# Holding the transfers on GpSimd's queue behind cells, cutting the casting copies into shorter runs, and adding identity products to the head of a matmul-GELU-matmul kernel

## The chip, the cores and the metric

The kernel runs on one core of one Trainium2 chip. The metric is the device time of one launch in microseconds (us), as the median of several launches. A core has five instruction streams that run beside each other: TensorE (PE in the profile, with its weight loads as PEld), VectorE (DVE), ScalarE (ACT), GpSimd (POOL) and SyncE (SP, which here issues DMA transfers alone). Each stream works off its own instructions in the order in which they stand, and waits for another stream or a transfer only where the instruction in front needs it.

## The reference

```python
def reference(x, w1, b1, w2):          # x 16x512x768, w1 768x3072, w2 3072x768, all float32
    y = np.matmul(x, w1) + b1
    y = 0.5 * y * (1.0 + erf(y / np.sqrt(2.0)))
    return np.matmul(y, w2).astype(np.float32)
```

All 16 x 512 = 8,192 rows of x go through both layers. The kernel computes in fp16 with fp32 sums.

## The kernel before

**Layers.** The first layer is computed transposed: weights stationary, rows of x moving, results as tiles of 128 hidden columns x 512 rows. GELU writes them as fp16, and each tile goes to a DRAM buffer `gd` (one per 512 rows, 16 in all). The second layer reads `gd` back and writes `out`. Both layers save products with a fixed bilinear scheme (the tables `P1_*` and `P2_*`): 20 products do the work of 24, and in exchange sums of parts of x and of the weights must be formed ahead, and products be added and subtracted behind. The sums of weight parts are formed by VectorE (`w1_ops`), the sums of x parts by VectorE, from the second block on also by GpSimd (`x_sums`, three adds of 512 elements each there), and the products are combined by VectorE and ScalarE (`unit`).

**Stages of the first layer.** The first 512 rows, and the first 512 hidden columns of the 1,536 rows after them, are worked off plainly, without the scheme (`plain_group`, four tiles of six matmuls, on line 634). Six of these nine groups run before the first unit, and this stretch is called the head here. Then come five blocks of 1,536 rows (`p1_block`). A block has six units, one for each 512 hidden columns; a unit has 20 products of three matmuls each (line 736), twelve results, twelve GELUs (line 503) and twelve stores to `gd` (line 509). The first unit of block 0 is done plainly in the head. A store's source is one of eight slots (`gst`); GELU can't write a tile before a slot is free.

**How x comes in.** The first 512 rows come as fp32 over SP's queue (line 401), are cast by ScalarE (line 349) and transposed by PE (line 486). The next 1,536 rows, block 0, come over GpSimd's queue, which casts them on the way (line 649, three transfers), and are also transposed by PE. For the blocks after that a transfer on GpSimd's queue casts 256 rows from x to `xd`, an fp16 copy in DRAM (line 675), and a transposing transfer on SP's queue reads `xd` into the core (line 688). Each block has six such pairs. The transposing transfer waits on SP's queue until its `xd` rows have landed, and the stores that stand behind it on that queue wait with it.

**How the weights come in.** The first 512 columns of w1 come over SP's queue behind the first rows of x, in four pieces; the other five groups of 512 columns come over GpSimd's queue, two transfers each (all on line 424). They are cast by ScalarE or VectorE. w2 is cast from DRAM to DRAM into `w2d` by eight transfers on GpSimd's queue (line 789, through the helper of line 675).

**What sets the order.** The kernel has a planner (`Sched`). Each piece of work is given with an estimate for each engine that may do it, with what it reads and with `after`, pieces that must come first *in the plan*. The planner runs through the whole program once and writes the instructions of each engine in the order of its plan. Real waits are set only where data, buffers or engines' results demand them. An `after` therefore orders the plan, but holds nothing on the chip: a transfer on GpSimd's queue whose inputs are there is issued as soon as the stream reaches it. The casts of block b+1 are planned from the starts of units 0, 1 and 2 of block b (`CAST_AT`), the transposing transfers from units 1, 2 and 3 (`TR_AT`).

```python
gate = [blk_units[b - 1][CAST_AT[y]][0]]
S.add({"POOL": 0.5}, lambda e, a=a: rows_cast(xd[a:a + 256, :], xf[a:a + 256, :]),
      makes=[c], work=2.7, after=gate)
```

Of the kernel before, what the change touches and what calls it, by code (L numbers as in the profile page):

```python
# [9 lines left out]
FP32 = mybir.dt.float32  # L10
FP16 = mybir.dt.float16
ACTF = mybir.ActivationFunctionType
ALU = mybir.AluOpType
P = 128
# [21 lines left out]
P2_XOUT = [(27, 1), (10, 1), (18, 1), (8, 1), (12, 1), (17, 1), (19, 1), (14, 1), (23, 1), (16, 1), (7, 1), (25, 1), (6, 1), (2, 1), (26, 1), (21, 1), (24, 1), (3, 1), (0, 1), (9, 1)]  # L36
P2_OPS = [('C', [(1, 0, 0, 0)], -1), ('C', [(1, 0, 0, 2)], -1), ('C', [(1, 0, 1, 0)], -1), ('C', [(1, 0, 1, 2)], -1), ('C', [(1, 0, 2, 0)], -1), ('C', [(1, 0, 2, 2)], -1), ('C', [(1, 0, 3, 0)], -1), ('A', [(1, 1, 6, 0), (1, 0, 2, 1)], -1), ('A', [(-1, 1, 7, 0), (1, 0, 3, 4)], -1), ('A', [(-1, 1, 4, 0), (1, 0, 1, 1)], -1), ('A', [(1, 1, 9, 0), (1, 0, 2, 4)], -1), ('A', [(-1, 0, 3, 1), (1, 1, 0, 0)], -1), ('A', [(-1, 1, 11, 0), (1, 0, 4, 0)], -1), ('A', [(1, 1, 2, 0), (1, 0, 0, 1)], -1), ('A', [(-1, 1, 13, 0), (1, 0, 1, 4)], -1), ('F', [(1, 1, 8, 0)], 0), ('A', [(1, 1, 5, 0), (-1, 0, 3, 3)], -1), ('A', [(1, 1, 16, 0), (1, 1, 8, 0)], 1), ('A', [(-1, 1, 3, 0), (-1, 0, 2, 3)], -1), ('A', [(1, 1, 18, 0), (1, 1, 10, 0)], 2), ('F', [(1, 1, 10, 0)], 3), ('A', [(1, 0, 3, 2), (-1, 1, 12, 0)], 4), ('A', [(-1, 1, 12, 0), (-1, 0, 0, 3)], 5), ('F', [(-1, 1, 14, 0)], 6), ('A', [(-1, 1, 1, 0), (1, 0, 1, 3)], -1), ('A', [(1, 1, 24, 0), (-1, 1, 14, 0)], 7)]

CAST_AT = (0, 0, 1, 1, 2, 2)
TR_AT = (1, 1, 2, 2, 3, 3)  # L40
PE_LAG = 0.28
LAG = 0.10
END = {"PE": 0.0, "DVE": 0.085, "ACT": 0.11, "POOL": 0.04, "SP": 0.0}
# [209 lines left out]
def kernel(  # L253
# [43 lines left out]
    def a16(off, n):  # L297
        return ar[:, off // 2: off // 2 + n]
# [54 lines left out]
            eng.tensor_scalar(out=o, in0=a, scalar1=-1.0, scalar2=None, op0=ALU.mult)  # L353

    ctx.enter_context(tc.manual_schedule())
    tiny = main.tile([P, 1], FP32, name="tiny")
    nc.vector.memset(tiny[:], 0.0)
    nc.scalar.activation(out=tiny[:], in_=tiny[:], func=ACTF.Gelu)
    make_identity(nc, ident[:])


    gs_slots = Pool()
# [116 lines left out]
    def transpose_tile(nat_v, nat_ap, dst_fn, dst_v, frees=()):  # L479
        bv = Val(bank)  # L480
        pt = S.add({"PE": 0.45}, None, reads=[nat_v], frees=list(frees), alloc=bv)

        def fn(e):
            o = ps[:, bv.slot, 0:384].bitcast(FP16)
            for kc in range(KC):
                nc.tensor.transpose(out=o[:, kc * P:(kc + 1) * P], in_=nat_ap(kc), identity=ident[:])  # L486
        pt.fn = fn

        def ev(e):
            i = ps[:, bv.slot, 0:384].bitcast(FP16).rearrange("p (k c) -> p k c", c=P)  # L490
            if e == "DVE":
                nc.vector.tensor_copy(out=dst_fn(), in_=i)  # L492
            else:
                nc.scalar.copy(out=dst_fn(), in_=i)  # L494
        return pt, {"DVE": 0.48, "ACT": 0.70}, ev, bv, dst_v
# [99 lines left out]
        return list(prod.values())  # L595


    b1v = Val(bank)

    def b1_tr(e):  # L600
        nc.tensor.transpose(out=ps[:, b1v.slot, 0:HC], in_=b1n, identity=identf[:])
# [6 lines left out]
    x0T = Val(xtr)  # L608
    first = True
    for s in range(4):  # L610
        pt, dur, ev, bv, dv = transpose_tile(
            x0v[s], lambda kc, s=s: a16(x0n.slot + s * 1536 + kc * 256, P),
            lambda s=s: a16(x0T.slot, 3072).rearrange("p (k r) -> p k r", r=512)[:, :, s * P:(s + 1) * P], x0T, frees=[x0n])
        S.add(dur, ev, reads=[bv], alloc=x0T if s == 0 else None, makes=[x0T], after=x0T.prods[:1])
# [25 lines left out]
    def plain_group(u, xT, row):  # L640
        return [plain_tile(u, q, xT, row) for q in range(4)]

    xt0 = (lambda: a16(x0T.slot, 3072).rearrange("p (k r) -> p k r", r=512), [x0T], [x0T])
    x1n = []
    for j in range(3):
        if j:
            w1_load(j, w1cast[1:2])
        v = Val()
        S.add({"POOL": 0.8}, lambda e, j=j: nc.gpsimd.dma_start(
            out=a16(O_XB + j * 6144, 3072).rearrange("p (s k) -> p s k", k=K), in_=xr[:, 4 + 4 * j:8 + 4 * j, :]),  # L650
            makes=[v], work=5.3, after=w1cast[1:2])
        x1n.append(v)
    plain_group(0, xt0, 0)
    w1_ops(0, S.pe_ideal + 5.0)
    x1done = []
    for j in range(3):
        for c in range(4):
            s = 4 * j + c
            pt, dur, ev, bv, dv = transpose_tile(
                x1n[j], lambda kc, s=s: a16(O_XB + s * 1536 + kc * 256, P),  # L660
                lambda j=j, c=c: x_third(0, j)[:, :, c * P:(c + 1) * P], xsv[0][j])
            x1done.append(pt)
            S.add(dur, ev, reads=[bv], makes=[xsv[0][j], xsv[0][3 + j]])
        if j:
            plain_group(j, xt0, 0)
        plain_group(0, (lambda j=j: x_third(0, j), [xsv[0][j]], []), 512 + 512 * j)
    w1_load(3, x1done[:1])


    blk_last = {}  # L670
# [1 line left out]

    def rows_cast(o, i):

        nc.gpsimd.dma_start(out=o.rearrange("(h r) c -> r h c", h=2), in_=i.rearrange("(h r) c -> r h c", h=2))  # L675

    def load_x(b):
        r0 = BLK[b]
        for y in range(6):
            j, z = divmod(y, 2)  # L680
            a = r0 + y * 256
            c = Val()
            gate = [blk_units[b - 1][CAST_AT[y]][0]]
            S.add({"POOL": 0.5}, lambda e, a=a: rows_cast(xd[a:a + 256, :], xf[a:a + 256, :]),
                  makes=[c], work=2.7, after=gate)
            after = [blk_units[b - 1][TR_AT[y] + (b == 1)][0]]
            after += blk_last[b - 2] if b >= 2 else x1done
            S.add({"SP": 0.45}, lambda e, a=a, z=z, j=j: nc.sync.dma_start_transpose(  # L688
                out=x_third(b, j)[:, :, z * 256:z * 256 + 256], in_=xd[a:a + 256, :]), reads=[c],
                makes=[xsv[b][j], xsv[b][3 + j]], after=after, work=2.2, late=3.0)  # L690
# [27 lines left out]
    def p1_block(b):  # L718
        r0 = BLK[b]
        dur = 3 * MM1  # L720
        xo = x_sums(b, S.pe_ideal, dur)
        blk_units[b] = []
        for u in range(6):
            if b == 0:
                if u == 0:
                    blk_units[b].append([x1done[-1]])
                    continue
                w1_ops(u, S.pe_ideal - 1.0)
                if u >= 3:
                    plain_group(u, xt0, 0)  # L730

            def mm(bk, i, first, lst, u=u):
                c, w, xx = P1_ORD[i]
                xa = xo[xx][1]()
                for kt in range(3):
                    nc.tensor.matmul(out=ps[:, bk, :], lhsT=w1_ap(u, w)[:, kt * P:(kt + 1) * P],  # L736
                                     rhs=xa[:, kt * 512:(kt + 1) * 512], start=(first and kt == 0),
                                     stop=(kt == 2), skip_group_check=True)

            def out_final(kind, tms, outi, tap, signed, reads, frees, u=u):  # L740
                q, j = divmod(outi, 3)
                return finish((reads, lambda: tap(tms[0])), u * 4 + q, r0 + j * 512, tms[0][0], frees)

            def frees_of(i, u=u):
                return [xo[P1_ORD[i][2]][0]] + ([wreg[u][P1_ORD[i][1] // 4]] if b == NBK - 1 else [])

            blk_units[b].append(unit(
                P1_ORD, P1_LEN, P1_OPS, 512, mm, dur, vpool,
                lambda i, u=u: [w1v[u][P1_ORD[i][1]], xo[P1_ORD[i][2]][0]], frees_of, out_final))
            if b == 0 and u < 3:  # L750
                w1_load(u + 3, blk_units[0][u - 1][:1])
        blk_last[b] = [t for p in blk_units[b] for t in p]


# [32 lines left out]
    w2dv = [Val()]  # L787
    for i in range(8):
        S.add({"POOL": 0.8}, lambda e, i=i: rows_cast(w2d[384 * i:384 * i + 384, :], w2[384 * i:384 * i + 384, :]),
              makes=w2dv, work=4.0, after=blk_units[1 + i // 3][3 + i % 3][:1])  # L790
    rawx = Pool([O_XB], heir=lambda t, s: [q.put(t, O_XB + 8192 * i) for i, q in enumerate(gset[:2])])
    gset = [Pool(), Pool(), g2slot]
    w2half = [[None, None] for _ in P2_WOUT]
# [162 lines left out]
```

## Time and profile before

| what | value |
|---|---|
| time, median of three runs | 904.99 us (901.28 to 909.65) |
| the profiled execution's own time | 907.87 us |
| its span, first to last instruction | 906.1 us |
| PE busy | 860.0 us (95%) |
| DVE / ACT / POOL busy | 621.0 / 427.9 / 107.4 us |
| first matmul of the units (line 736) | at 63.94 us |
| first matmul of the second layer (line 901) | at 478.86 us |
| mean granted TensorE clock | 0.994 |

The page of the profile gives each engine's busy time, and the span in 40 slices of 22.65 us each, one digit for the busy share in tenths. The times of the profiled execution are a little above the median of the runs shown; sums are made against its own time. The timeline lists instructions of one engine in order: start, time, what, and in brackets how long the engine was idle before and what ended the wait.

### The profile page before, as it was taken

The page shows a single profiled execution, that of the slowest core. Times are in us where ns is not written, and L with a number is a line of the kernel's source. Part 1 is how long each engine was busy: PE and PEld are TensorE (multiplying, and loading weights), DVE is VectorE, ACT ScalarE, POOL GpSimd, SP SyncE. Part 2 cuts the span into 40 slices and gives each one's busy share as a digit, 9 for nine tenths or more (in the row PEclk, how much of TensorE's full clock was granted, in tenths as well). Part 3 has the DMA queues.
Part 4 walks back from the last instruction along what each step waited for, and adds up shares of the span by engine and source line. Part 5 has one row for each costly group of instructions (what it writes and reads, how often), then busy time and mean ns, then how long its engine had stood idle before and what let it go on. Part 6 is the DMA issues. An engine that isn't in the chain of part 4 may idle for free.

```text
span 906.1 us, 13480 instructions
## 1 busy us (share of the span) xinstructions
PE 860.0 (95%) x4613; PEld 449.3 (50%) x4613; DVE 621.0 (69%) x1027; ACT 427.9 (47%) x727; POOL 107.4 (12%) x116
## 2 busy tenths in 40 slices
PE   3799999999989998999998999999999998999997
PEld 1344444444434443444445666666566665666564
DVE  0489648558646865689876977777677676777763
ACT  3897866777767776777872212111211111121121
POOL 4200015035304610620000000000000000000000
PEclk9999999999999999999999999999999999999999
DMA  9985557974996599464689566545456654555611
GB/s 268 338 231 146 151 152 161 246 204 133 202 226 169 154 226 235 143 218 136 203 255 336 177 209 209 168 171 188 154 162 204 209 176 150 164 188 165 204 71 70
DMA packets 141369, 171.56 MB, mean 189 GB/s; under 512 B 47709, under 2 KB 132725, under 8 KB 135157
## 3 DMA queue, kind: packets, MB, share of 16 engines
q1 hardware_dynamic: 127872, 146.32, 51.8%
q0 software_dynamic: 13392, 24.38, 12.6%
q8 instruction: 36, 0.59, 0.3%
q14 instruction: 33, 0.26, 0.1%
q10 hardware_dynamic: 36, 0.01, 0.0%
HBM read 102.25 MB, written 89.65 MB: 212 GB/s over the span
## 4 chain that ended last, share of the span: by engine, by line
PE 76%; DMA 8%; DVE 7%; ACT 4%; issue 3%; SPq 1%; ACTq 0%; DVEq 0%
PE ps L901 43%; PE ps L736 29%; DVE ar L344 4%; PE ps L634 3%; DVE vt L344 3%; DMA ar<-gd 3%; DMA gd<-ar 3%; DMA ar<-in_w_dram 3%; ACT ar L503 2%; SPq L688 1%; ACT vt L349 1%; ACT ar L494 0%; ACT ar L349 0%; SPq L424 0%; SPq L509 0%
## 5 line engine op out<-in xcount | busy, mean ns | idle before, releaser
L901 PE MATMUL ps<-ar 128*128 128x384 f16 x2560 | 418.3, 327 | 6.4 <-DVE vt L344 4.0
L736 PE MATMUL ps<-ar 128*128 128x512 f16 x1740 | 382.1, 380 | 15.3 <-ACT vt L349 7.9
L901 PEld LDWEIGHTS <-ar 128*128 128x128 f16 x2560 | 251.0, 98 | 173.8 <-issue 6.1
L344 DVE TENSOR_TENSOR ar<-ar 128x1024 f16<-128x1024 f16 (+2 forms) x402 | 260.7, 671 | 49.9 <-ACT ar L349 24.5
L736 PEld LDWEIGHTS <-ar 128*128 128x128 f16 x1740 | 170.4, 98 | 226.4 <-issue 25.5
L349 ACT ACTIVATE vt<-ps 128x512 f32<-128x512 f32 (+1 forms) x228 | 122.1, 544 | 267.2 <-PE ps L901 245.1
L344 DVE TENSOR_TENSOR vt<-vt,ps 128x512 f32<-128x512 f32 (+1 forms) x254 | 163.3, 643 | 93.4 <-ACT vt L349 41.7
L344 DVE TENSOR_TENSOR vt<-ps,vt 128x512 f32<-128x512 f32 (+1 forms) x225 | 144.3, 641 | 94.4 <-ACT vt L349 39.6
L503 ACT ACTIVATE ar<-vt,b1t 128x512 f16<-128x512 f32 x232 | 162.3, 716 | 76.3 <-DVE vt L344 61.0
L503 ACT ACTIVATE ar<-ps,b1t 128x512 f16<-128x512 f32 x152 | 102.2, 686 | 11.3 <-DMA gd<-ar 4.1
L344 POOL TENSOR_TENSOR ar<-ar 128x512 f16<-128x512 f16 x63 | 74.3, 1212 | 256.1 <-PE ps L736 142.0
L349 ACT ACTIVATE ar<-vt 128x384 f32<-128x384 f32 x48 | 25.0, 520 | 98.0 <-DVE vt L344 98.0
L634 PE MATMUL ps<-ar 128*128 128x512 f16 x216 | 53.2, 406 | 12.1 <-ACT ar L349 10.5
L349 ACT ACTIVATE ar<-ar 128x384 f16<-128x384 f16 (+4 forms) x53 | 39.9, 794 | 18.3 <-DMA ar<-in_w_dram 13.5
L634 PEld LDWEIGHTS <-ar 128*128 128x128 f16 x216 | 21.6, 102 | 41.3 <-ACT ar L349 13.5
L342 DVE SCALAR_TENSOR_TENSOR vt<-vt,ps 128x512 f32<-128x512 f32 (+1 forms) x45 | 28.6, 636 | 2.7 <-PE ps L901 0.7
L344 DVE TENSOR_TENSOR ar<-vt 128x384 f32<-128x384 f32 x48 | 26.8, 558 | 1.7
L342 DVE SCALAR_TENSOR_TENSOR ar<-vt,ps 128x384 f32<-128x384 f32 x16 | 8.9, 554 | 21.7 <-PE ps L901 21.7
L675 POOL DMA_DIRECT2D xd<-in_x_dram x24 | 16.3, 685 | 13.6 <-DMA ar<-in_w_dram 9.1
L486 PE MATMUL ps<-ident,ar 128*128 128x128 f16 x96 | 8.1, 241 | 3.0 <-ACT ar L349 3.0
L492 DVE COPY ar<-ps 128x768 f16<-128x768 f16 x5 | 2.8, 556 | 11.8 <-PE ps L486 11.6
L344 DVE TENSOR_TENSOR ar<-ps,vt 128x384 f32<-128x384 f32 x16 | 8.9, 557 | 0.5
(22 smaller groups left out, 43.0 us busy)
## 6 DMA issues: line engine op xcount, KB each, us to landing
gd<-ar SPq DMA_DIRECT2D x384, 128.0 KB, 2.1
ar<-gd SPq DMA_DIRECT2D x48, 1024.0 KB, 5.5
out_dram<-ar SPq DMA_DIRECT2D x128, 192.0 KB, 2.0
xd<-in_x_dram POOLq DMA_DIRECT2D x24, 384.0 KB, 12.3
ar<-in_w_dram POOLq DMA_DIRECT2D x10, 768.0 KB, 21.9
w2d<-in_w_dram POOLq DMA_DIRECT2D x8, 576.0 KB, 18.8
ar<-w2d SPq DMA_DIRECT2D x8, 576.0 KB, 5.3
ar<-w2d SPq DMA_DIRECT2D x8, 384.0 KB, 6.7
```

The source lines that it names most:

```text
L342: eng.scalar_tensor_tensor(out=o, in0=a, scalar=-1.0, in1=b, op0=ALU.mult, op1=ALU.subtract)
L344: eng.tensor_tensor(out=o, in0=a, in1=b, op=ALU.add if op == "+" else ALU.subtract)
L349: nc.scalar.activation(out=o, in_=a, func=ACTF.Copy, scale=float(sg))
L486: nc.tensor.transpose(out=o[:, kc * P:(kc + 1) * P], in_=nat_ap(kc), identity=ident[:])
L492: nc.vector.tensor_copy(out=dst_fn(), in_=i)
L503: ft = S.add({"ACT": 0.61}, lambda e: nc.scalar.activation(out=a16(g.slot, 512), in_=src[1](), func=ACTF.Gelu, bias=b1t[:, t:t + 1], scale ...
L634: nc.tensor.matmul(out=ps[:, bv.slot, :], lhsT=raw_w1(u, 2 * q + kc // 3)[:, kc % 3, :], rhs=xT[0]()[:, kc, :], start=(kc == 0), stop=(kc ...
L675: nc.gpsimd.dma_start(out=o.rearrange("(h r) c -> r h c", h=2), in_=i.rearrange("(h r) c -> r h c", h=2))
L688: S.add({"SP": 0.45}, lambda e, a=a, z=z, j=j: nc.sync.dma_start_transpose(out=x_third(b, j)[:, :, z * 256:z * 256 + 256], in_=xd[a:a + 25 ...
L736: nc.tensor.matmul(out=ps[:, bk, :], lhsT=w1_ap(u, w)[:, kt * P:(kt + 1) * P], rhs=xa[:, kt * 512:(kt + 1) * 512], start=(first and kt == ...
L901: nc.tensor.matmul(out=ps[:, bk, 0:NB], lhsT=xa[:, j, :], rhs=a16(w2half[w][j // 4].slot + (j % 4) * W1T, NB), start=(first and j == 0), s ...
```

## The change

There are five edits.

1. **Cells.** A small tile `tiny` gets 34 columns. `gate(after)` plans a one-element memset on VectorE behind the product given in `after`, and a one-element copy on GpSimd that reads that cell. The copy is a real wait on GpSimd's stream; the memset is a place in VectorE's order. 24 casts of x and eight casts of w2 each get such a pair ahead of them.
2. **Places.** `place(b, i)` names product i of block b, counted through its units. The six casts of a block are planned from products 0, 10, 20, 30, 40 and 50, the transposing transfers from products 14 to 64 (20 later for block 1), and the casts of w2 from products 60 to 90 of blocks 1 and 2.
3. **Runs.** `rows_cast` walks the copy as three column groups of 256 elements, outermost, then rows. Before, it walked pairs of rows with whole rows of 768 elements.
4. **The head's loads.** The transfers on GpSimd's queue in the head (three of x, now all ten of w1 directly behind) stand behind a one-element copy on GpSimd that reads the last of the four cast tiles of the first 512 rows.
5. **Identity products.** `awake(n, ns)` puts n matmuls of the identity with itself (128 x 128 x 128) on PE: 12 at the very start, 16, 4, 6 and 10 ahead of the four transposed tiles of the first rows, 22 ahead of the first plain group, and 12 ahead of each third of block 0.

```diff
-CAST_AT = (0, 0, 1, 1, 2, 2)
-TR_AT = (1, 1, 2, 2, 3, 3)
+CAST_AT = (0, 10, 20, 30, 40, 50)
+TR_AT = (14, 24, 34, 44, 54, 64)
...
+    def gate(after):
+        i = next(cells)
+        v = Val()
+        S.add({"DVE": 0.07}, lambda e: nc.vector.memset(tiny[0:1, i:i + 1], 0.0), after=after, makes=[v])
+        return S.add({"POOL": 0.07}, lambda e: nc.gpsimd.tensor_copy(out=tiny[0:1, 33:34], in_=tiny[0:1, i:i + 1]),
+                     reads=[v])
...
+    def awake(n, ns):
+        v = Val(bank)
+        def fn(e):
+            for _ in range(n):
+                nc.tensor.matmul(out=ps[:, v.slot, 0:P], lhsT=ident[:], rhs=ident[:], start=True, stop=True)
+        S.add({"PE": n * ns / 1000}, fn, alloc=v, frees=[v])
...
+    awake(12, 107)
...
     for s in range(4):
+        awake((16, 4, 6, 10)[s], 107)
...
+    x1g = [S.add({"POOL": 0.07}, lambda e: nc.gpsimd.tensor_copy(
+        out=tiny[0:1, 33:34], in_=a16(x0n.slot + 3 * 1536, 1)[0:1, :]), reads=[x0v[3]], after=x0c[6:7])]
     for j in range(3):
         if j:
-            w1_load(j, w1cast[1:2])
+            w1_load(j, x1g)
...
-            makes=[v], work=5.3, after=w1cast[1:2])
+            makes=[v], work=5.3, after=x1g)
+    awake(22, 60)
     plain_group(0, xt0, 0)
     for j in range(3):
+        awake(12, 60)
...
-    w1_load(3, x1done[:1])
+    w1_load(3, x1g)
+    w1_load(4, x1g)
+    w1_load(5, x1g)
...
-        nc.gpsimd.dma_start(out=o.rearrange("(h r) c -> r h c", h=2), in_=i.rearrange("(h r) c -> r h c", h=2))
+        nc.gpsimd.dma_start(out=o.rearrange("r (a c) -> a r c", a=3), in_=i.rearrange("r (a c) -> a r c", a=3))
+    def place(b, i):
+        u = blk_units[b][i // 20]
+        return u[min(i % 20, len(u) - 1)]
...
-            gate = [blk_units[b - 1][CAST_AT[y]][0]]
+            held = [gate([place(b - 1, CAST_AT[y])])]
...
-                  makes=[c], work=2.7, after=gate)
-            after = [blk_units[b - 1][TR_AT[y] + (b == 1)][0]]
+                  makes=[c], work=2.7, after=held)
+            after = [place(b - 1, TR_AT[y] + 20 * (b == 1))]
...
-            if b == 0 and u < 3:
-                w1_load(u + 3, blk_units[0][u - 1][:1])
...
-              makes=w2dv, work=4.0, after=blk_units[1 + i // 3][3 + i % 3][:1])
+              makes=w2dv, work=4.0, after=[gate([place(1 + i // 4, 60 + 10 * (i % 4))])])
```

## The prediction, made before the changed kernel was run

> **What bounds the kernel now.** I read the page first, then PE's waits, then the timelines of PE, GpSimd and SP around the longest of those waits. The page (busy times, and two rows of the 40 slices):
>
> ```profile
> PE 860.0 (95%) x4613; PEld 449.3 (50%) x4613; DVE 621.0 (69%) x1027; ACT 427.9 (47%) x727; POOL 107.4 (12%) x116
> ...
> PE   3799999999989998999998999999999998999997
> ...
> DMA  9985557974996599464689566545456654555611
> ```
>
> PE sets the time: only some 46 us of the span are not its work, and a change that removes no matmul can win no more. The low digits stand in the first two slices (45 us) and at the very end; the DMA engines are full in just the first slices. The rest is lost in small pieces, and PE's list of waits (waiting line, releaser, us in all, times, longest) names the two that matter:
>
> ```profile
> PE ps L634 <- ACT ar L349: 10.5, 4, 4.0
> PE ps L736 <- ACT vt L349: 7.9, 5, 3.5
> ```
>
> The first is the head. Its timeline on PE:
>
> ```profile
> 19.53 4.02 PE L634 MATMUL ps<-ar 128*128 128x512 f16 x9 [2.89 <-ACT ar L349]
> 23.71 1.46 PE L634 MATMUL ps<-ar 128*128 128x512 f16 x3 [0.16 <-ACT ar L349]
> 28.69 3.80 PE L634 MATMUL ps<-ar 128*128 128x512 f16 x9 [3.52 <-ACT ar L349]
> ...
> 35.36 5.34 PE L634 MATMUL ps<-ar 128*128 128x512 f16 x24 [1.52 <-ACT ar L494]
> ...
> 63.94 5.37 PE L736 MATMUL ps<-ar 128*128 128x512 f16 x24
> ```
>
> The first plain group is drawn out from 15.17 to 32.3 us, waiting for casts of weights; from 35 us on PE hardly waits. What the casts wait for is in the chain that ended last (start, us, what): the fourth piece of the first weights, issued at 4.52 us, took 23.25 us to land.
>
> ```profile
> 4.52 23.25 DMA ar<-in_w_dram
> ```
>
> At 1.65 us GpSimd's queue had begun to issue x of block 0 and later weights, and both queues share the DMA engines. The second wait is two stalls of 3.20 us (before 260.65) and 3.45 us (before 345.05). SP's timeline at the first of them, and GpSimd's before it:
>
> ```profile
> 245.80 11.10 SPq L688 DMA_TRANSPOSE ar<-xd  x2
> 256.99 6.79 SPq L509 DMA_DIRECT2D gd<-ar  x10
> ```
>
> ```profile
> 230.24 4.06 POOL L675 DMA_DIRECT2D xd<-in_x_dram  x6
> 234.29 1.54 POOL L675 DMA_DIRECT2D w2d<-in_w_dram  x2
> ```
>
> Eight casts are issued in 5.6 us and occupy the DMA engines until 256 us; two transposing transfers behind them hold SP for 11.10 us instead of some 3; no store leaves; the eight slots fill; GELU, then PE stop. The second stall has the same shape (a hold of 11.40 us from 329.94). So a hold of SP costs PE about its length less 7.9 us (11.10 - 3.20, 11.40 - 3.45).
>
> **The head's loads (edit 4).** GpSimd's first transfer moves from 1.65 us to after the first cast of the fourth x tile. SP's eight loads then run nearly alone. The first x piece landed at 4.08 us. By the trace's packets each engine gives an x piece 8 of 121 ns (0.97 us) and a weight piece 24 of 46 ns (1.10 us), so x would land by 4.1 to 7.0 and the weights by 8.1 to 11.4 us. Then the chain is ScalarE's: with its casts (0.44 and 0.84 us) and evacuations (0.79) in the built order, the fourth x tile's first half is cast at about 9.4, x is evacuated by 13.1 and the last weights are cast at 14.8 us. PE does the group's 24 matmuls in 13.1 to 18.5 us (5.34 by the row above), not until 32.3. GpSimd's first x third starts at 9.5: 0.9 us to issue, 32 packets of 134 ns per engine (4.3 us), about 2 us beside: it lands near 17, in time. Later thirds land 4.4 + 4 us apart by the same rates (25, 33), ahead of PE. From there PE's own chain: three times 12 identity products (0.7 us), 24 transposes (1.50), once the gap for the evacuation (1.52), and 24, 48 and 48 matmuls (5.3, 10.5, 10.5): 18.5 + 2.1 + 4.5 + 1.5 + 26.3 = 52.9 us for the first matmul of the units, against 63.94: 11.0 less. What could be late next is ScalarE: it did 38 us of work between 14.8 and 63.94 (its windows show 9.5 to 10.0 of 10 us from 30 to 60), which now must fit in 38.1 us. I take 1.5 us for that: **-9.5 us** (bounds -3, if ScalarE and VectorE, 97% busy from 56 to 90 us, carry most of it back, and -12).
>
> **Identity products (edit 5).** 106 in all. The first 70 stand where PE waits for x or ScalarE. The 36 before the thirds stand on the chain and are in the sum above (2.1 us; a 128-row transpose takes 62 ns). What they may win is the clock: nine matmuls took 3.80 us at 28.69 (422 ns each) and 24 took 5.34 (222 ns) once PE was busy. The chain above counts the warm rate throughout. The Trainium skill (TensorE: Matmul & The Clock Gate, section Part 1) gives a gate that opens after some 3.4 us of activity and closes after as much idleness, and 107 against 56 ns for a product of this size. It agrees with these rows; nothing here rests on it.
>
> **Cells (edit 1).** 32 memsets on VectorE (the memset of line 357 took 0.06 us), 1.9 us of an engine that is 69% busy: +0.5 us, bounds 0 and +2. GpSimd's copy waits for VectorE, and behind it stand the casts and the x sums that GpSimd forms (3 x 1.2 us each, 24 of them now), whose readers are products on PE. In the built order the sums of a block stand together ahead of the next block's first cast, with one held w2 cast among them in blocks 2 and 3, so the holds can't delay them much.
>
> **Casts and transposing transfers (edits 1 to 3).** Gone: the burst, and with it 3.20 + 3.45 = **-6.65 us**. New: each transposing transfer follows its own cast closely, on a stream with all the stores behind it. In the built orders of blocks 2 and 3 the casts follow VectorE's combining instruction 6, 6, 12, 18, 24 and 30 of the block's 72, and the transposing transfers follow store 12, 14, 21, 26, 33 and 38 of 72. A block takes about 81 us (1.125 us per store): 7 to 10 us apart, and a few more because stores trail the combining. The cost hangs on how fast one cast lands. Low end: alone on all engines, like the first of a burst (230.24 to 235.84, 314.42 to 318.95 us: 4.5 to 5.6 us): no wait, the -6.65 stands. High end: three engines. The copy's outermost count is now 3 where it was 128, and a row of this page shows that the count matters:
>
> ```profile
> q0 software_dynamic: 13392, 24.38, 12.6%
> ...
> q10 hardware_dynamic: 36, 0.01, 0.0%
> ```
>
> Queue q10 carried b1 alone: 24 rows, so 24 packets, and 12 markers of its end: 12 engines, a divisor of 24, not 16. With three engines each gets 256 runs of 1,024 bytes: 46 ns as SP's packets of that size take, 11.8 us, stretched to 15 to 17 by the stores (eight packets of 46 ns per engine each 1.125 us, a third of it), plus 2: a landing of 17 to 19 us. Then holds are 17 to 19 less 9 to 12 plus 2 to 3 for the transfer, 7 to 13 us, on both sides of the 7.9 us that cost nothing. I take one stall of the measured size, **+3.3 us**, as nearest to both ends; ends 0 and +40 (below).
>
> The Trainium skill speaks against this edit: DMA: Bandwidth & Descriptors, in Rules for kernel authors, confines a transfer to as many engines as its outermost count if that is under 16, and under Why a DMA increments its semaphore by 16 and not by 1 it lets GpSimd's queue take three neighbours in turn. By it the high end would apply to every cast. The before-trace shows it for b1's queue only.
>
> **Sum.** 907.87 - 9.5 - 6.65 + 3.3 + 0.5 = 895.5 us for the profiled execution; that execution lay 2.9 us over its median, so **893 us** as a median of runs. The second layer, 427 us of the span, isn't touched.
>
> **Rivals.**
> *The transposing transfers wait (slower).* All casts on three engines: the pair at the start of blocks 2 and 3 holds SP for 19 - 9 + 2 x 3 + a few stores = 16.5 us, 8.6 us of stall, and each later second transfer some 3 to 4: 15 us a block, 10 in block 1, about 40. 895.5 - 3.3 + 40 - 2.9 = 929. It is slower than before once such stalls exceed 15.7 us (9.5 + 6.65 - 0.5). For it: the outermost count, SP's order. Against it: a stall moves later transfers away from their casts, and three engines at a time leave 13 free. Chance 0.28.
> *All engines take part.* No new stall: 892.2 - 2.9 = 889. Chance 0.15.
> *The head doesn't move.* ScalarE and VectorE, full from 30 to 90 us, give the gain back: 893 + 6.5 = 900, with half-size new stalls 905. Chance 0.17.
> *The holds don't hold.* Cells carry no wait on PE, only VectorE's order; if VectorE runs ahead, casts bunch up as before: 893 + 3.3 = 896; this lies within the forecast's own spread.
> *The forecast*, 888 to 898: 0.37. The remaining 0.03 is for casts that all land on the same three engines (ten casts of 12 us and more in a block of 81 us: above 1,000).
>
> **How the numbers follow.** The range runs from 886 (head -12, no new stall, less) to 930, the waiting rival's price, and leaves out some 0.15. A difference of under 1% (9 us) can hardly be told from none here. Faster by over 1% (below 896): most of the forecast and the case of all engines, 0.48. Within 1%: the head that doesn't move and mild waits, 0.22. Slower: 0.30.
>
> **What would show it.** Right: the first unit matmul near 54 us; the four weight pieces landed by 13; no gap of over 1 us on line 767 (line 736 now); SP's transposing transfers at 1.3 to 3 us each. Wrong: a cast's time from issue to landing at 15 us or more with transposing transfers that begin only then; long waits of GELU on stores; GpSimd's sums late for PE; ScalarE full with PE waiting for it before 54 us.

## The result and the profile after

The changed kernel takes **1027.5 us** (median; 1018.8 to 1045.8) against 905.5 us before in the same comparison: a ratio of 1.1315, 95% interval 1.1219 to 1.1411. It is 13% slower. The ratio leaves out the longest of the four executions, 1045.8 us, which ran in a slower state. The forecast was 893 us, the range ended at 930.

The profiled execution took 1028.46 us, span 1026.4. In the changed file the unit's matmuls stand on line 767 (736 before), GELU on 513 (503), the stores on 519 (509), the casts on 702 (675), the transposing transfers on 719 (688), the cell's memset and copy on 367 and 368. From its page: busy times, three rows of the 40 slices (25.7 us each), GpSimd's DMA queue (packets, MB, share of 16 engines), the unit's matmuls (count, busy and mean ns, idle before), and the median time from issue to landing of the stores and the casts:

```profile
PE 895.0 (87%) x4719; PEld 462.3 (45%) x4719; DVE 653.5 (64%) x1061; ACT 429.2 (42%) x722; POOL 158.3 (15%) x158
...
PE   8987798677595674766999999999999999999998
...
PEclk9998999788797888788999999999999999999999
...
q0 software_dynamic: 151632, 24.86, 24.9%
...
L767 PE MATMUL ps<-ar 128*128 128x512 f16 x1740 | 418.0, 401 | 120.9 <-ACT vt L349 72.3
...
gd<-ar SPq DMA_DIRECT2D x384, 128.0 KB, 6.4
...
xd<-in_x_dram POOLq DMA_DIRECT2D x24, 384.0 KB, 24.3
...
w2d<-in_w_dram POOLq DMA_DIRECT2D x8, 576.0 KB, 33.4
```

The same matmuls, stores and casts on the page of the kernel before:

```profile
L736 PE MATMUL ps<-ar 128*128 128x512 f16 x1740 | 382.1, 380 | 15.3 <-ACT vt L349 7.9
...
gd<-ar SPq DMA_DIRECT2D x384, 128.0 KB, 2.1
...
xd<-in_x_dram POOLq DMA_DIRECT2D x24, 384.0 KB, 12.3
```

The first slice is filled now (8, where a 3 stood) and the second half of the span is as before: the whole loss stands between 50 and 525 us, in the four blocks during which casts run. PE's idle time before the unit's matmuls rose from 15.3 to 120.9 us, and the matmuls themselves from 382.1 to 418.0 us of busy time. The casts take 24.3 us (x) and 33.4 us (w2) to land, where they took 12.3 and 18.8, and a store 6.4 us (2.1). GpSimd's queue moves nearly the same bytes (24.86 MB, 24.38 before) in eleven times the packets (13,392 before).

By the trace, blocks 0 to 3 take 99.1, 114.8, 127.9 and 130.8 us, where they took 83.1, 81.1, 84.1 and 81.4. Block 4, which has no casts beside it, takes 81.3 (82.7). So blocks 0 to 3 lose 142.9 us. Against that stand 13.4 us gained in the head, 1.4 in block 4 and 7.7 in the second layer (421.9 us, 429.6 before), which the change doesn't touch: 120.3 us between the spans of 1026.4 and 906.1.

PE's list of waits of the same execution (waiter, releaser, us in all, times, longest):

```profile
PE ps L767 <- ACT vt L349: 72.3, 19, 10.3
PE ps L767 <- ACT ar L513: 24.1, 15, 8.5
PE ps L767 <- POOL ar L344: 21.7, 9, 8.7
```

The copies on line 349 are ScalarE's, of products that are added later. They stand in ScalarE's stream behind GELUs (line 513), and a GELU waits for a free slot.

One of the stalls, in the timelines of SP, ScalarE and PE:

```profile
170.63 3.83 SPq L719 DMA_TRANSPOSE ar<-xd  x1
174.55 4.32 SPq L519 DMA_DIRECT2D gd<-ar  x7
```

```profile
184.40 0.69 ACT L513 ACTIVATE ar<-ps,b1t 128x512 f16<-128x512 f32 x1 [9.47 <-DMA gd<-ar]
```

```profile
167.81 8.80 PE L767 MATMUL ps<-ar 128*128 128x512 f16 x40
185.13 11.08 PE L767 MATMUL ps<-ar 128*128 128x512 f16 x41 [8.53 <-ACT ar L513]
```

The transposing transfer on SP's queue waited for its cast, issued at 152.32 us and landed at 170.49, and no store left between 163.18 and 174.55 us, a hold of 11.3 us. By then every slot was taken. (There are eight slots only in block 0; from block 1 on the kernel takes three more out of a tile that is free by then, and at the stalls of both kernels eleven tiles are written and not yet landed.) The first store behind the hold, issued at 174.55 us, took 9.76 us to land. Only then could GELU write its slot (184.40 us), and PE, which had run until 176.61 us, stood for 8.53 us. On the page's chain the landing of stores has 14% of the span. The stall costs more than its length. The same stretch in windows (window, us, PE busy, weight loads, then the granted clock; the last two columns, on DMA, aren't used):

```profile
168.00:176.00 8.00, 8.00 (x38) 3.63 (x37) 1.00 1.16 89
185.10:188.60 3.50, 3.46 (x9) 1.23 (x9) 0.50 1.52 93
190.00:193.00 3.00, 3.00 (x15) 1.37 (x14) 1.00 1.35 62
```

Behind this stall the clock is at 0.50 for 4.2 us (until 189.36 us); in the 3.5 us of the second row nine matmuls take the time of 17. In this trace each of the 17 stalls of over 2 us among the units is followed by 2.7 to 6 us at 0.50, and none of the seven between 1 and 2 us is.

The head did what was forecast, and more. PE's timeline of the changed kernel:

```profile
50.50 5.78 PE L767 MATMUL ps<-ar 128*128 128x512 f16 x26
```

The first unit matmul is at 50.50 us, not at 63.94.

### The profile page after: what moved, and what is told of

Its sections match the earlier page's. It is cut to its first block, busy times and chain, and to the rows that moved or that the text cites. A ratio compares the mean times of both kernels' runs of the same rounds, so it can differ in the third digit from the quotient of the medians.

```text
span 1026.4 us, 13794 instructions
## 1 busy us (share of the span) xinstructions
PE 895.0 (87%) x4719; PEld 462.3 (45%) x4719; DVE 653.5 (64%) x1061; ACT 429.2 (42%) x722; POOL 158.3 (15%) x158
## 3 DMA queue, kind: packets, MB, share of 16 engines
q0 software_dynamic: 151632, 24.86, 24.9%
## 4 chain that ended last, share of the span: by engine, by line
PE 62%; DMA 18%; issue 8%; DVE 4%; ACT 4%; SPq 2%; POOL 1%; ACTq 0%; DVEq 0%; POOLq 0%
PE ps L930 41%; PE ps L767 17%; DMA gd<-ar 14%; PE ps L655 4%; ACT ar L513 2%; DMA xd<-in_x_dram 2%; DVE vt L344 2%; DVE ar L344 1%; SPq L719 1%; ACT vt L349 1%; SPq L519 1%; POOL ar L344 1%; DMA ar<-gd 1%; ACT ar L349 1%; PE ps L496 0%
## 5 line engine op out<-in xcount | busy, mean ns | idle before, releaser
L767 PE MATMUL ps<-ar 128*128 128x512 f16 x1740 | 418.0, 401 | 120.9 <-ACT vt L349 72.3
L767 PEld LDWEIGHTS <-ar 128*128 128x128 f16 x1740 | 176.9, 102 | 361.4 <-issue 166.6
L930 PEld LDWEIGHTS <-ar 128*128 128x128 f16 x2560 | 250.4, 98 | 166.7 <-DVE ar L344 1.2
L344 DVE TENSOR_TENSOR ar<-ar 128x1024 f16<-128x1024 f16 (+2 forms) x399 | 287.7, 744 | 39.3 <-ACT ar L349 11.9
L349 ACT ACTIVATE vt<-ps 128x512 f32<-128x512 f32 (+1 forms) x225 | 119.1, 542 | 259.3 <-PE ps L930 239.1
L344 POOL TENSOR_TENSOR ar<-ar 128x512 f16<-128x512 f16 x72 | 85.4, 1218 | 92.6 <-DMA ar<-xd 82.8
L655 PE MATMUL ps<-ar 128*128 128x512 f16 x216 | 47.8, 379 | 2.0 <-ACT ar L504 1.2
L702 POOL DMA_DIRECT2D xd<-in_x_dram x24 | 38.6, 1608 | 33.2 <-issue 26.3
L349 ACT ACTIVATE ar<-ar 128x384 f16<-128x384 f16 (+4 forms) x50 | 37.7, 800 | 0.0
L655 PEld LDWEIGHTS <-ar 128*128 128x128 f16 x216 | 21.0, 98 | 26.8 <-issue 1.3
L368 POOL COPY tiny<-tiny 1x1 f16<-1x1 f16 x32 | 6.4, 200 | 159.8 <-DVE tiny L367 159.6
L702 POOL DMA_DIRECT2D w2d<-in_w_dram x8 | 17.1, 2142 | 66.5 <-DMA gd<-ar 59.4
L613 PE MATMUL ps<-ident 128*128 128x128 f16 x106 | 9.4, 252 | 1.4 <-POOL identf masks.py:197 1.4
## 6 DMA issues: line engine op xcount, KB each, us to landing
xd<-in_x_dram POOLq DMA_DIRECT2D x24, 384.0 KB, 24.3
w2d<-in_w_dram POOLq DMA_DIRECT2D x8, 576.0 KB, 33.4
```

The lines of the kernel that those rows point to most:

```text
L344: eng.tensor_tensor(out=o, in0=a, in1=b, op=ALU.add if op == "+" else ALU.subtract)
L349: nc.scalar.activation(out=o, in_=a, func=ACTF.Copy, scale=float(sg))
L368: return S.add({"POOL": 0.07}, lambda e: nc.gpsimd.tensor_copy(out=tiny[0:1, 33:34], in_=tiny[0:1, i:i + 1]), reads=[v])
L613: nc.tensor.matmul(out=ps[:, v.slot, 0:P], lhsT=ident[:], rhs=ident[:], start=True, stop=True)
L655: nc.tensor.matmul(out=ps[:, bv.slot, :], lhsT=raw_w1(u, 2 * q + kc // 3)[:, kc % 3, :], rhs=xT[0]()[:, kc, :], start=(kc == 0), stop=(kc ...
L702: nc.gpsimd.dma_start(out=o.rearrange("r (a c) -> a r c", a=3), in_=i.rearrange("r (a c) -> a r c", a=3))
```

## The experiments

Ratios are to the kernel before, run beside it on the same chip, with 95% intervals; its medians there were 903.2 to 905.8 us. Diffs are against the changed kernel unless another is named.

### The shape of the casts

**Old shape, all else kept.**

```diff
-        nc.gpsimd.dma_start(out=o.rearrange("r (a c) -> a r c", a=3), in_=i.rearrange("r (a c) -> a r c", a=3))
+        nc.gpsimd.dma_start(out=o.rearrange("(h r) c -> r h c", h=2), in_=i.rearrange("(h r) c -> r h c", h=2))
```

> The changed kernel, with the old shape of the casts (outermost 128, whole rows); cells, one-by-one order, head and identity products stay. Theory A (three engines: the outermost count of 3 keeps each cast on few engines, and its long transfer slows the stores and the transposing transfers): casts land in 5 to 8 us, transposing transfers in about 4.4 us again, stores in about 2, no stall of over 2 us on the unit matmuls, first unit matmul still at 50.5, blocks of 81 to 84 us, time 885 to 897. Theory B (the one-by-one order and the cells cost whatever the shape of the casts): blocks stay at 100 us and more, time above 980.

904.6 us, ratio 1.001 (0.9979 to 1.0041). From its page:

```profile
L767 PE MATMUL ps<-ar 128*128 128x512 f16 x1740 | 386.8, 383 | 32.5 <-DVE vt L344 22.8
...
gd<-ar SPq DMA_DIRECT2D x384, 128.0 KB, 4.1
...
xd<-in_x_dram POOLq DMA_DIRECT2D x24, 384.0 KB, 7.2
```

This one line is worth 123 us: the stalls for stores are gone. But the time is 8 us over theory A's range, with another wait on top: VectorE's, taken up below.

**Short runs, but 128 outermost.**

```diff
+        nc.gpsimd.dma_start(out=o.rearrange("(h r) (a c) -> r a h c", h=2, a=3), in_=i.rearrange("(h r) (a c) -> r a h c", h=2, a=3))
```

> The changed kernel, with casts in the same runs of 256 elements, but an outermost count of 128. Theory A: all 16 engines take part, 48 packets of 59 ns on each (2.8 us), landing in 5 to 8 us, no packets of 4 bytes beyond the markers, GpSimd's issue of a cast still longer than before (some 1.6 us), time 885 to 900. Theory C: 27,648 short packets as in the changed kernel, so time stays above 960.

903.2 us, ratio 0.9954 (0.9914 to 0.9994). From its page:

```profile
q0 software_dynamic: 31824, 24.38, 15.9%
...
xd<-in_x_dram POOLq DMA_DIRECT2D x24, 384.0 KB, 7.1
```

It is 3 us over theory A's range, with the same wait for VectorE as with whole rows. The runs of 256 elements cost nothing (903 us, 905 with whole rows): theory C falls. The packets are 31,824 against 13,392 with whole rows; the difference of 18,432 is just the 27,648 short ones in place of 9,216 long ones. The changed kernel has 119,808 more, 13/3 of 27,648, and in its trace these are packets of 4 bytes: to every three packets with data on three engines come 13 without, one for each engine that has no part.

**Four and eight outermost, whole rows.**

```diff
+        nc.gpsimd.dma_start(out=o.rearrange("(r h) c -> h r c", h=4), in_=i.rearrange("(r h) c -> h r c", h=4))
```

> The changed kernel, with casts of whole rows (1,536 bytes written, 3,072 read) but an outermost count of 4. Theory A: four engines, 64 rows of 134 ns on each for a cast of x, 8.6 us, 10 to 14 us to landing, packets of 4 bytes again (12 per row step, some 27,600); the stores wait on those four engines; time 910 to 980, between the other two. Theory C (the short runs cost, not the engines): long runs, so as fast as the old shape, 885 to 897, landing in 5 to 8 us.

> The changed kernel with casts of whole rows and an outermost count of 8. Eight engines per cast: 32 rows of 134 ns each, 4.3 us, landing in 7 to 10 us; packets of 4 bytes: 8 for 8 of data, 10,752 plus 720 markers. By the series three (1027 us), four (989), 128 (904.6): 915 to 945.

989.3 us, ratio 1.0934 (1.0880 to 1.0988), 9 us over the range for four, and 932.4 us, ratio 1.0311 (1.0278 to 1.0344), in the range for eight. GpSimd's queue in the first, then in the second:

```profile
q0 software_dynamic: 41040, 24.49, 13.8%
```

```profile
q0 software_dynamic: 22608, 24.42, 13.1%
```

With four, 27,648 more than with 128 outermost: 12 for every four of the 9,216 packets. With eight, 9,216 more: eight for every eight (I had counted 10,752, having taken x's other transfers in). Long runs don't save the casts: what sets the price comes with the outermost count. That count sets two things together, the number of engines that carry a cast and the packets of 4 bytes on the others. With four, these packets took only 357 us of the 16 engines' time, 2% of their span, and the kernel still lost 85 us to the old shape. That speaks for the fewer engines as the larger part there, without showing it. In the changed kernel they took 1,838 us (11%), and these runs don't separate their part. Median landing of x's casts, and the time: outermost count 3: 24.3 us, 1027; 4: 14.2 us, 989; 8: 8.3 us, 932; 128: 7.2 us, 905.

**Old order with the new shape** (the kernel before with edits 3 to 5 alone).

> The kernel with the head's edits alone (891.2 us), and the casts in runs of 256 elements with the outermost count of 3; no cells, the casts go off in bursts of eight as before the change. Theory A (few engines per cast, each with its own packets, whatever the order): a burst has 8 casts on groups of three engines, some 34 engine-us of data for a cast of x and 51 for one of w2, so 306 us over 16 engines or 19 us at the very best, 30 to 45 us to landing for the last ones; the pairs of transposing transfers wait for them and time is 950 to 1050. Rival (only the one-by-one order exposes the long landing, since in a burst the casts run side by side): 891 to 905.

998.9 us, ratio 1.1032 (1.0976 to 1.1088), in the range of theory A; the head alone is at 0.9864 (below). So neither cells nor the one-by-one order are needed for the loss; the shape makes it alone.

**Transposing transfers later.**

```diff
-TR_AT = (14, 24, 34, 44, 54, 64)
+TR_AT = (24, 34, 44, 54, 64, 74)
```

> The changed kernel (casts on three engines), with every transposing transfer ten places (about 11 us) later in SP's order. If the price is SP held by a transposing transfer that waits for its own cast (TR behind a landing of 24 us): the holds shrink by up to 11 us each, time falls to 930 to 980. If the price is that stores share engines with the casts and land in 6.4 us in place of 2.1, however long SP waits: 1005 to 1035.

994.2 us, ratio 1.0994 (1.0935 to 1.1052): between the two. It is 33 us less by the medians and 29 by the ratios; stores still land in 5.8 us, and PE still stands 93.5 us before the unit's matmuls. Ten places later don't remove the holds: transposing transfers held SP for 139 us in all here, 156 in the changed kernel and 59 in the kernel before (each counted from the end of the DMA issue ahead of it to the end of its own). So 33 us is the least that they cost, and their full share isn't separated.

What slows the stores can be counted in the traces. Between the first cast's issue and the last one's landing, I sorted the stores by what was in flight when they were issued (median us to landing; number of stores):

| in flight | before | changed | sums on VectorE, old shape |
|---|---|---|---|
| nothing | 1.7 (126) | 1.7 (29) | 1.7 (59) |
| one cast | 2.9 (16) | 5.0 (16) | 4.8 (87) |
| two casts | 6.8 (7) | 6.6 (79) | 6.6 (11) |
| three or more | 8.2 (48) | 8.2 (26) | none |
| a transposing transfer alone | 2.7 (24) | 1.8 (4) | 2.5 (9) |
| one and a cast or more | none | 10.0 (77) | 5.8 (62) |

A cast in flight makes a store slow in every kernel, and a transposing transfer beside casts slower still. What the shape changes is how many stores leave in such company: 182 of 231 beside two or more casts, or beside a transposing transfer and a cast, against 73 of 228 in the last column and 55 of 221 before. The mean number of casts in flight in that stretch doesn't tell it: 1.94 in the changed kernel and 0.81 in the last column's, but 1.37 in the kernel before, where the casts come in bursts.

The slow landing is what ScalarE waits for. Of its 19 waits of over 1 us for a store in the changed kernel, 109.4 us in all, 102.5 us passed while that store was already under way. Why a store is slow there is argued only: SP's packets of 1,024 bytes, nearly all of them of stores, took 52.8 ns on average (49.0 before), which is nearly the same, so they wait between other packets. The packets of 256 bytes of the transposing transfers took 62.7 ns (22.3 before). A store has markers on all 16 engines, 16 per transfer by the trace; that it ends with its slowest engine is argued too.

### The head

**The head's edits alone** (edits 4 and 5 on the kernel before).

> The kernel before, with the head's loads and the identity products of the change alone; casts, cells and transposing transfers as before the change. First unit matmul at 50 to 51 us as in the changed kernel. If the head's gain reaches the end: 905.5 less 13.4 = 892, with the two stalls of some 3 us still there at the start of the third and fourth block. If ScalarE and VectorE, full from 30 to 90 us, give it back: 898 to 905, with waits on GELU in the first block.

891.2 us, ratio 0.9864 (0.9827 to 0.9901); first unit matmul at 50.9 us. The head's gain, 13.0 us at the first unit matmul, reaches the end nearly whole (12.3 us by the ratio).

**The same without identity products.**

```diff
-            for _ in range(n):
+            for _ in range(0):
```

> The kernel before with the head's edits (891.2 us), without the 106 identity products. If they only stand in PE's waits and 36 of them on the chain (2.1 us): first unit matmul 2 us earlier or at the same time, 889 to 892. If they keep PE's clock up: the plain group's matmuls at 400 ns and more while PE waits for x and weights, first unit matmul 1 to 4 us later, 892 to 896.

892.5 us, ratio 0.9868 (0.9836 to 0.9900), first unit matmul at 50.8: no difference that can be measured, neither for them nor against them. Without them the plain groups' matmuls take 50.1 us in all and not 47.8, and the second group starts at 22.2 us and not at 20.8; by the start of the fifth (40.4 us, 40.5 with them) nothing of it is left.

### VectorE's wait

In the kernel with the old shape, PE stood 10.4 us for VectorE at 213 and again at 309 us. GpSimd's and VectorE's timelines ahead of the first:

```profile
190.04 3.38 POOL L344 TENSOR_TENSOR ar<-ar 128x512 f16<-128x512 f16 x3 [1.69 <-PE ps L767]
...
194.05 0.81 POOL L702 DMA_DIRECT2D w2d<-in_w_dram  x1 [0.27 <-DMA gd<-ar]
194.88 16.66 POOL L344 TENSOR_TENSOR ar<-ar 128x512 f16<-128x512 f16 x15
```

```profile
196.61 15.75 DVE L344 TENSOR_TENSOR ar<-ar 128x1536 f16<-128x1536 f16 x1
```

A sum that VectorE does in 0.95 us elsewhere took 15.75 us, beside 14 of GpSimd's 15 sums, and ended 0.8 us after the last of them. VectorE's steps that have an operand in PSUM are not touched: they take 0.69 us beside GpSimd's sums as well. The same is in the changed kernel, at 263.37 (14.32 us; this one got in 1 us before the last of the 15 sums ended) and 403.98 (12.96). Before the change no VectorE sum took over 1.8 us; GpSimd's sums stood in groups of 3, 6 and 9 with waits between.

**No cells.** (The casts keep their places in the plan, and wait for nothing.)

```diff
-            held = [gate([place(b - 1, CAST_AT[y])])]
+            held = [place(b - 1, CAST_AT[y])]
...
-              makes=w2dv, work=4.0, after=[gate([place(1 + i // 4, 60 + 10 * (i % 4))])])
+              makes=w2dv, work=4.0, after=[place(1 + i // 4, 60 + 10 * (i % 4))])
```

(This and the next four have the old shape too.)

> The changed kernel with the old shape of the casts, and without cells: GpSimd issues its casts as soon as its stream reaches them. Against the same with cells (904.6 us, with two stalls of 10.4 us on PE behind a sum of VectorE that took 15.75 us beside 15 sums of GpSimd back to back). Theory D (the holds made GpSimd late, so that its sums went off back to back and kept VectorE's sum out): no VectorE sum over 3 us, no stall of 10 us; the casts come in bursts again and cost up to 2 x 3 us; 885 to 894. Theory E (the run of 15 sums stands in the order anyway, holds or not): the two stalls stay, 900 to 908.

908.3 us, ratio 1.0038 (1.0018 to 1.0058). The casts come in bursts again in this run, so its time alone decides nothing. But theory D falls as I had put it: nothing holds GpSimd, and yet VectorE's timeline shows

```profile
195.07 10.05 DVE L344 TENSOR_TENSOR ar<-ar 128x1536 f16<-128x1536 f16 x1
```

beside nine of GpSimd's sums. The cells aren't needed for the wait: it comes with where the sums stand in the order.

**A memset of one element between the sums.**

```diff
+                    if e == "POOL":
+                        nc.gpsimd.memset(tiny[0:1, 33:34], 0.0)
                     comb(e, a16(v.slot + 2 * h, step), op, fa()[:, h:h + step], fb()[:, h:h + step])
```

> The changed kernel with the old shape of the casts, and a memset of one element on GpSimd ahead of each of its sums of 512 elements (72 more instructions of under 0.2 us). If VectorE's sum is kept out for as long as GpSimd's sums follow each other without a gap, an instruction between them that reads no operand lets VectorE in after one or two sums: VectorE's longest sum falls from 15.75 to under 4 us and the time to 884 to 892. If VectorE is kept out for the whole group whatever stands between: stalls of 10 us or more stay, 904 to 910.

909.0 us, ratio 1.0051 (1.0030 to 1.0071); VectorE's sum takes 16.82 us. A memset between, which reads nothing, didn't let it in.

**The w2 casts earlier.**

```diff
-              makes=w2dv, work=4.0, after=[gate([place(1 + i // 4, 60 + 10 * (i % 4))])])
+              makes=w2dv, work=4.0, after=[gate([place(1 + i // 4, 25 + 10 * (i % 4))])])
```

> The changed kernel with the old shape of the casts, cells kept, but the second weights' casts held at places 25, 35, 45 and 55 of a block in place of 60, 70, 80 and 90, so that none stands among GpSimd's sums (in the built order GpSimd then keeps 3 sums ahead of the third and fourth block in place of 18, VectorE takes the other five tiles, 0.95 us each). Theory D: no VectorE sum over 3 us, no burst, so 905.5 less 13.4 less 6.65 = 885, plus some 2 for VectorE's extra sums: 884 to 890. Theory E': one-by-one casts cost something else: 898 to 908.

913.6 us, ratio 1.0094 (1.0066 to 1.0122). VectorE's long sums are gone, as expected, but the casts of x and w2 now alternate too closely, and SP's timeline shows a transposing transfer held for 6.70 us among them:

```profile
246.34 6.70 SPq L719 DMA_TRANSPOSE ar<-xd  x1
```

It took 21.4 us to land. PE stood 20.2 us for ScalarE's copies (line 349), which stand behind GELUs that wait for stores, and the time is above both theories' ranges. So this run can't tell the price of the sums.

**All sums of x on VectorE.**

```diff
-            prev = [S.add({"DVE": dve_tt(1536), "POOL": 3 * pool_tt(512)} if b else {"DVE": dve_tt(1536)}, fn, reads=[va, vb], alloc=v,
+            prev = [S.add({"DVE": dve_tt(1536)}, fn, reads=[va, vb], alloc=v,
```

> The changed kernel with the old shape of the casts (904.6 us), and all sums of x on VectorE: GpSimd has casts and cells alone. If the two stalls of 10.4 us come from GpSimd's runs of sums that keep VectorE's sum out: no VectorE sum over 3 us, those stalls gone, VectorE gets some six sums of 0.95 us more per block, 5 of its 29 us between two blocks: 884 to 894. If the stalls belong to something else that stands at that place (x that lands late for its sums): PE still waits 10 us for VectorE before the third and fourth block, 900 to 908.

**880.4 us, ratio 0.9715** (0.9684 to 0.9746), the fastest of all and below the expected range, though VectorE forms 24 more sums. From its page:

```profile
L767 PE MATMUL ps<-ar 128*128 128x512 f16 x1740 | 382.0, 380 | 11.0 <-ACT ar L513 7.1
...
gd<-ar SPq DMA_DIRECT2D x384, 128.0 KB, 4.2
```

Stores that land in 4.2 us leave PE nearly no wait here. Against the old shape with GpSimd's sums (1.001) the stalls are worth 3.0%: in the profiled spans 906.3 - 884.3 = 22.0 us.

**The same, casts in a burst.**

```diff
-CAST_AT = (0, 10, 20, 30, 40, 50)
-TR_AT = (14, 24, 34, 44, 54, 64)
+CAST_AT = (0, 0, 0, 0, 0, 0)
+TR_AT = (20, 20, 40, 40, 60, 60)
...
+              makes=w2dv, work=4.0, after=[gate([place(1 + i // 3, 0)])])
```

> The kernel with all sums of x on VectorE (880.4 us), but all eight casts of a block released by cells at the first place of a block, and the transposing transfers in pairs as before the change. If the one-by-one order is worth the two stalls that I had counted at 6.65 us: 886 to 891, with stalls of 3 us before the third and fourth block. If the order is worth nothing, and the whole gain of that kernel over 891.2 is that GpSimd's sums are gone: 878 to 883.

904.0 us, ratio 0.9996 (0.9976 to 1.0017), slower than either range. SP's timeline has the pair of transposing transfers that the kernel before had, 13.46 us long:

```profile
243.70 13.46 SPq L719 DMA_TRANSPOSE ar<-xd  x2
```

Only the order of the transfers differs from the kernel at 880.4: it is worth 2.8%. The burst is not quite that of before (nine casts, issued 2 to 10 us into the block, and a longer hold), so for the kernel before I estimate 13 us (the ratios 0.9864 and 0.9715, where the sums' place differs as well) to 25 us (0.9996 and 0.9715).

**The changed kernel with all sums on VectorE** (casts on three engines).

> The changed kernel, casts on three engines, with all sums of x on VectorE. If the price of GpSimd's runs of sums adds to that of the three engines: 1027 less 24 = 1003, no VectorE sum over 3 us, PE's waits for GpSimd (21.7 us) gone. If both hide behind one another (PE waits for GELU at that place anyway): 1018 to 1030.

1012.8 us, ratio 1.1205 (1.1176 to 1.1233), between the two. Without GpSimd's sums PE still stands 113.5 us before the unit's matmuls (120.9 with them): the stalls behind the sums and those behind the stores hide each other in part.

## Why the prediction was wrong, step by step

By the ratios the time adds up as 1 - 0.0136 (the head) - 0.0149 (the burst gone, with all sums on VectorE) + 0.0295 (the sums where the plan puts them) + 0.1305 (the shape of the casts) = 1.1315, or some -12, -13, +27 and +118 us.

**The head (edit 4), -9.5: right, under-sized.** The four weight pieces landed at 9.4 to 12.6 us, the chain was 2.4 us shorter than I had it (50.5, not 52.9), and the 1.5 us for ScalarE weren't due. Together with the identity products it gives 1.36%, 12.3 us, and 1.32% without them: just past the far bound of -12. The rival "the head doesn't move" falls.

**Identity products (edit 5), nothing: right.** 0.9864 with, 0.9868 without.

**Cells (edit 1), +0.5: the memsets right, the places not priced.** The 32 memsets took 1.7 us in all. I asked whether holds make GpSimd's sums late, and the run without cells has VectorE's wait too. What costs is the new order (edit 2): it puts one w2 cast behind the first three sums and the other 15 sums behind it in one piece, and while such a piece runs VectorE gets, mostly, no sum of its own in. That cost 22 us (spans) to 27 us (ratios) in the old shape; in the prediction it has no term. I had VectorE's sums and GpSimd's in the rows before me, and priced each alone. The Trainium skill (SBUF — State Buffer, Who interferes with whom) has the rule that I didn't look up: a VectorE instruction with both inputs in SBUF contends with a GpSimd instruction that reads SBUF, and the later of the two waits until the first has finished. The runs show the contention, but a longer wait than that rule: through 9 to 14 instructions (10.05 to 15.75 us), and with a memset between them as well (16.82). The kernel without GpSimd's sums shows the way out.

**The burst gone, -6.65: right in sign, two to four times too small.** I counted the two stalls alone. Between the burst and the one-by-one order PE's idle time before the unit's matmuls falls from 25.2 to 11.0 us and their busy time from 386.3 to 382.0. Most of it is three stalls of 5.30, 4.88 and 1.88 us, with 6.8 us at half clock behind each of the first two. That is 16 us between the profiled spans; the medians lie 24 apart, and the rest stays open.

**Casts and transposing transfers (edits 1 to 3), +3.3 between 0 and +40: this step failed.** It should have read +118 us (the ratios 1.1315 and 1.001) to +123 (the medians 1027.5 and 904.6), and with all sums on VectorE +135 (1.1205 and 0.9715); the range's end for it was +40. Three terms were off.

- *Which end.* I had worked out 17 to 19 us of landing for three engines, and took a value near the low end because I weighed a stall's shift and "13 engines free". The cast issued at 152.32 us, alone for its first 10.5 us, took 18.18 us, so three engines was the end to take. That the number matched is partly luck: a packet of 256 elements took 59 ns and not 46, which gives 15.1 us a cast where I had stretched 11.8 to as much. The Trainium skill (DMA: Bandwidth & Descriptors, Rules for kernel authors) says that an outermost count under 16 confines a transfer to at most that many engines. These runs agree: 3, 4, 8 and 128 outermost give 24.3, 14.2, 8.3 and 7.2 us. That others of the 16 stay free is no comfort: in the changed kernel they get the 119,808 packets of 4 bytes, and a store has markers on all 16.
- *How casts overlap.* 18 us each, issued mostly 3 to 16 us apart, run two at a time: landing 24.3 us for x, 33.4 for w2. GpSimd issued the third and the fourth cast of w2 only after an older one had landed (244.57 after a landing at 244.26, 259.14 after 258.83), and the sums behind it were late for PE. I had no such wait in the sum. GpSimd's timeline:

```profile
244.57 2.13 POOL L702 DMA_DIRECT2D w2d<-in_w_dram  x1 [16.11 <-DMA gd<-ar]
246.72 3.37 POOL L344 TENSOR_TENSOR ar<-ar 128x512 f16<-128x512 f16 x3
...
259.14 2.16 POOL L702 DMA_DIRECT2D w2d<-in_w_dram  x1 [8.93 <-DMA gd<-ar]
261.32 17.38 POOL L344 TENSOR_TENSOR ar<-ar 128x512 f16<-128x512 f16 x15
```

- *What it costs PE.* I priced holds of SP by "length less 7.9 us". That price was read off where the first store behind a hold landed in 2.3 us. By it the changed kernel's holds, 1.4 to 11.3 us long, would cost some 11 us (an estimate), where PE's idle time before the unit's matmuls grew by 105.6. The holds help to fill the slots, but the wait is that of the stores behind them, which take 5 to 10 us to land while casts are in flight. And I priced stalls at their length, where each of over 2 us is followed by 2.7 to 6 us at half the clock: 36 us of longer matmuls over the 382.1.

**The rivals.** The waiting transposing transfers, at 929, had the direction. The run with later ones shows at least 33 us of the 123 for them; their full share isn't separated, and their price left out the slow stores. "The same three engines every time, above 1,000" had the size but not the mechanism: a cast alone has 3 to 4 us of packets with data under way in each us (159 to 164 us), three at once 8 to 11 (168 to 171 us), so they take different engines. "All engines take part" falls with the landing of 24.3 us; "the holds don't hold" is not what happened either, for the casts are mostly 3 us and more apart.

## What to carry to other kernels

In these runs a DMA with an outermost count of 3, 4 or 8 landed later the smaller the count, and its price lay not in its own landing but in that of the transfers that were in flight beside it. Put 128 outermost, as the runs at 903 and 905 us did; the length of the runs made no difference there. Price a cast queue by what leaves beside transfers in flight, not by the longest hold of the queue behind it. Before work on GpSimd is moved, look what VectorE does beside it: sums of two SBUF tiles on both engines mostly didn't run side by side here.

## What the runs showed of the hardware

- A transfer on GpSimd's queue with an outermost count of 3, 4 or 8 puts a packet of 4 bytes on each engine without data for every round of packets with data: 119,808, 27,648 and 9,216 of them here, and none (beyond 16 per transfer) with 128.
- A cast of x takes GpSimd longer to issue with short runs: 1.07 us with 128 outermost and 1.60 with three, against 0.68 us with 128 outermost and whole rows; with whole rows it is 0.85 us for four and 0.66 for eight.
- In the changed kernel never more than three casts of x, or two of w2, were in flight (2,304 runs of 256 elements either way). Eleven times GpSimd issued the next one only 0.31 us after an older one had landed, with its whole stream waiting behind it.
- A VectorE sum of two SBUF tiles can wait for a whole run of GpSimd sums. Not always: before the change one got in after a single sum (215.80 us, 1.70 us long). What decides it stays open.
